# A two-layer hybrid trunk on one core: F16 halves for the value products, an earlier weight split, and memory queries as a seven-product set

## The chip, the core and the metric

The kernel runs on one core of a Trainium2 chip. The time is the device time of one execution in microseconds (us). TensorE (PE) multiplies matrices, with its weight loads as a stream of their own (PEld); VectorE (DVE), ScalarE (ACT) and GpSimd (POOL) do the elementwise work; SyncE (SP) issues the transfers. Each engine works through its own queue in order, and the engines wait for each other by semaphores.

## The reference, cut to what matters

Two residual layers over 2048 tokens of width 1024, then a last RMSNorm. Layer 0 is gated linear attention (GLA), layer 1 dilated window attention; each also attends over 256 memory rows, multiplies by a SiLU gate and projects back.

```
for i in range(DEPTH):                                   # DEPTH = 2
    h = rmsnorm(x, norm_w[i])
    if i % 2 == 0: mix, q_mem, gate = gla_mixer(h, ...)   # 4 heads, Dk = 96, Dv = 192
    else:          mix, q_mem, gate = dilated_mixer(h, w_in_b[j])
    mem_o = memory_attention(q_mem, mem_n, w_memkv[i])    # 4 heads of 64
    branch = concatenate([mix, mem_o]) * silu(gate)
    x = x + branch @ w_out[i]
...
# gla_chunked, chunks of 64 tokens:
q_in, k_in, k_out = q * exp(b), k * exp(-b), k * exp(b_last - b)
A = where(causal, q_in @ k_in.T, 0)
o = A @ v + q_in @ S;   S = exp(b_last) * S + k_out.T @ v
```

## The kernel before

**Products.** A large product takes both operands as a high and a low F16 half and adds three F16 products into one bank (`mm3`: hi x hi, hi x lo, lo x hi; lines 181 to 183). Weights are scaled by a power of two, cast to the high half on ACT, and the low half is the difference on DVE. `proj` does this over the 8 slices of the width (24 matmuls). `F32` matmuls appear in the trace as two instructions.

**Prologue and the loop of layer 0.** The tokens come in 16 blocks of 128 (two chunks each). The prologue loads and splits the input weights (wv2, wv0, wv1, wk1, wqk, wq0; `lw1_steps`) and does the projections of blocks 0 and 1. The loop then runs over b, and in step b: `gla_o(b)` multiplies AT by v and qs by the state S (both f32, lines 644 and 645, into one bank per head pair) and elb (the k_out of the formula) by v for the new state (line 650); the projections of block b+2 (`pre_gl`, `pre_v`, `pre_k`, `pre_qk`, `pre_q`) fill TensorE; `gla_T` and `gla_A` transpose q and k of block b+1 and multiply them (line 635), and a masked copy (`copy_predicated`, line 637) writes AT. `pre_la`, `pre_elb` make cumulated gates with F32R products against `tri` and `rev` (lines 569 to 578) and per-chunk sums against `ind` (f32, line 580). Inside the loop the order on PE, DVE, ACT and POOL is that of the code (`manual_schedule`). Side work is cut into steps, taken in turn by `tick`: the norm of the next block (`ga_steps`), the memory rows (`mem_rows`: two scaled row blocks, line 686, each transposed, line 691), the memory keys and values (`mem_steps`, line 710, in a bank of the projections' pool ps_mm), and in later blocks the weights of the second pass (`w2_steps`).

**Second pass of layer 0.** Over the 16 blocks again: memory query, memory attention (lines 260, 261, 286, 288, with transposes by DMA into mp and mpt), gate, the branch (transposed by DMA into bT), the output projection (`ps_o<-wo,bT`), and the next layer's normed input into h2T (`a2_h2`). In front of the first block the output projection's weights are loaded in four quarters and split. Order here is a scheduler's. `a2_sums` makes combinations S1 to S4 of h2T and stores them.

**Start of layer 1.** From here PE follows the order of the code again. A pair of column blocks of w_in_b is multiplied either directly (`proj_t`: 24 matmuls of 512 columns for a quarter of the tokens) or as a seven-product set (Strassen-like: seven products of 12 matmuls in place of eight for a half of the tokens and 256 columns, with weight combinations T1 to T4 on POOL and the stored S1 to S4 as the other operand). Memory queries take eight `proj_t` (`memq`), gate column block 4 four (`gate4`); between them stand the loads of S, the last sums and the first set's norm, combinations and splits. Then twelve sets follow.

## Time and profile before

| quantity | value |
|---|---|
| runs | 2552.51, 2547.39, 2550.93 us; median 2550.93 us |
| the profiled execution's own time | 2551.06 us |
| its span | 2549.3 us |
| TensorE busy | 2472.3 us, 97% of the span |
| DVE, ACT, POOL busy | 1583.3, 1331.8, 577.5 us |
| prologue, loop of layer 0, second pass's start | 0 to 66, 66 to 437, 437 to 520 us |
| second pass, start of layer 1, sets | 520 to 866, 866 to 966, 966 to 1440 us |
| attention with its projections, end | 1440 to 2350, 2350 to 2549 us |

A row of a timeline gives the start, the time, the engine, line, operation, output and inputs, and in brackets how long the engine sat idle before it and what released it. A row by line gives busy time, mean ns of one, and idle time ahead with its releaser. Stage bounds in the table are where TensorE's work passes from one to the next.

### The profile page before, as it was taken

What the parts mean: (1) busy time and instruction counts of PE and PEld (TensorE: products, weight loads), DVE (VectorE), ACT (ScalarE), POOL (GpSimd) and SP (SyncE); (2) the same over time, 40 slices, a digit from 0 to 9 for tenths busy, and PEclk for the clock granted to TensorE, in tenths of its full rate; (3) what the DMA queues carried; (4) which work ended last, traced back from release to release, by engine and by line L of the source; (5) the groups of instructions that cost most, each with busy time, mean ns of one, the idle gap of its engine ahead of it and who ended that gap; (6) DMA issues with size and microseconds to landing.
All of it is one profiled execution on the core that took longest, in us unless ns stands there. A gap on an engine that the chain in (4) does not pass through costs nothing.

```text
span 2549.3 us, 44543 instructions
## 1 busy us (share of the span) xinstructions
PE 2472.3 (97%) x16801; PEld 1653.3 (65%) x16801; DVE 1583.3 (62%) x3563; ACT 1331.8 (52%) x2905; POOL 577.5 (23%) x471
## 2 busy tenths in 40 slices
PE   7999999999999899999999999999999999998998
PEld 5888988788888744444544455555555555554898
DVE  6444554666875765655655455677776767768643
ACT  6434653544544545755555455556565655555322
POOL 0000000011210223455543012133242323323100
PEclk9999999999999999999999999999999999999999
DMA  6223432456666654568773324376575756748752
GB/s 239 79 86 105 136 112 69 133 145 156 173 166 133 158 187 119 157 162 188 167 201 120 121 56 112 90 169 164 132 183 118 183 133 163 166 124 216 233 180 98
DMA packets 623627, 371.71 MB, mean 146 GB/s; under 512 B 443874, under 2 KB 555956, under 8 KB 623028
## 3 DMA queue, kind: packets, MB, share of 16 engines
q1 hardware_dynamic: 623412, 368.87, 54.7%
q8 instruction: 131, 2.15, 0.4%
q14 instruction: 84, 0.69, 0.1%
HBM read 185.74 MB, written 95.86 MB: 110 GB/s over the span
## 4 chain that ended last, share of the span: by engine, by line
PE 78%; DVE 7%; DMA 6%; ACT 3%; issue 3%; SPq 1%; POOL 1%; DVEq 0%; ACTq 0%; POOLq 0%
PE ps_mm L183 15%; PE ps_mm L181 15%; PE ps_mm L182 15%; PE ps_x L183 6%; PE ps_x L181 6%; PE ps_x L182 6%; PE ps_mm L710 1%; DMA mpt<-stg 1%; PE ps_o L181 1%; PE ps_o L183 1%; PE ps_o L182 1%; PE ps_g L181 1%; PE ps_g L183 1%; PE ps_g L182 1%; PE ps_g L650 1%
## 5 line engine op out<-in xcount | busy, mean ns | idle before, releaser
L181 PE MATMUL ps_mm<-h2T,w 128*128 128x512 f16 x1112 | 423.4, 381 | 4.9 <-ACT w L1138 4.6
L183 PE MATMUL ps_mm<-h2T,w 128*128 128x512 f16 x1112 | 422.7, 380 | 0.6 <-DVE w L1142 0.6
L182 PE MATMUL ps_mm<-h2T,w 128*128 128x512 f16 x1112 | 423.0, 380 | 0.0
L181 PE MATMUL ps_mm<-w,hT 128*128 128x256 f16 (+1 forms) x1408 | 386.0, 274 | 7.8 <-ACT w L429 5.8
L183 PE MATMUL ps_mm<-w,hT 128*128 128x256 f16 (+1 forms) x1408 | 385.7, 274 | 0.0
L182 PE MATMUL ps_mm<-w,hT 128*128 128x256 f16 (+1 forms) x1408 | 385.6, 274 | 0.0
L183 PEld LDWEIGHTS <-w 128*128 128x128 f16 x1952 | 191.5, 98 | 233.7 <-issue 3.3
L181 PEld LDWEIGHTS <-w 128*128 128x128 f16 x1952 | 191.6, 98 | 216.7 <-ACT w L1138 5.2
L182 PEld LDWEIGHTS <-w 128*128 128x128 f16 x1952 | 191.6, 98 | 215.9 <-issue 8.4
L175 POOL TENSOR_TENSOR ph<-pm,ph 128x512 f16<-128x512 f32 (+2 forms) x144 | 162.5, 1128 | 630.7 <-ACT ph L174 427.9
L181 PE MATMUL ps_x<-h2T,w 128*128 128x512 f16 x552 | 210.0, 380 | 1.3 <-DVE c L1366 1.3
L182 PE MATMUL ps_x<-h2T,w 128*128 128x512 f16 x552 | 209.8, 380 | 0.0
L183 PE MATMUL ps_x<-h2T,w 128*128 128x512 f16 x552 | 209.7, 380 | 0.0
L1555 ACT ACTIVATE pm<-pm,st,cols 128x256 f32<-128x256 f32 (+1 forms) x288 | 156.1, 543 | 74.5 <-DVE st L1548 73.7
L175 POOL TENSOR_TENSOR stg<-mp,stg 128x512 f16<-128x512 f32 x16 | 19.5, 1217 | 725.7 <-ACT stg L174 725.7
L1544 DVE CUSTOM_DVE_ANT_0 pm<-ps_g,mw 128x256 f32<-128x256 f32 (+1 forms) x288 | 92.9, 359 | 98.3 <-PE ps_g L183 97.8
L181 PEld LDWEIGHTS <-hT 128*128 128x128 f16 x1408 | 138.2, 98 | 21.5 <-issue 2.2
L182 PEld LDWEIGHTS <-hT 128*128 128x128 f16 x1408 | 138.2, 98 | 20.1 <-issue 2.5
L183 PEld LDWEIGHTS <-hT 128*128 128x128 f16 x1408 | 138.1, 98 | 17.2
L1504 ACT ACTIVATE rx<-rw 128x512 f16<-128x512 f32 x36 | 33.9, 940 | 114.8 <-DVE rw L1503 114.8
L1488 ACT ACTIVATE rx<-ps_mm 32x512 f32<-32x512 f32 x96 | 56.1, 584 | 58.7 <-PE ps_mm L183 25.4
L174 ACT ACTIVATE ph<-pm 128x512 f16<-128x512 f32 (+2 forms) x144 | 77.3, 537 | 4.6
(625 smaller groups left out, 5925.3 us busy)
## 6 DMA issues: line engine op xcount, KB each, us to landing
stg<-in_w_in_b SPq DMA_DIRECT2D x80, 256.0 KB
v<-vd SPq DMA_DIRECT2D x72, 256.0 KB
fb<-fd SPq DMA_DIRECT2D x24, 768.0 KB
od<-osb SPq DMA_DIRECT2D x68, 256.0 KB
og<-od SPq DMA_DIRECT2D x68, 256.0 KB
x<-in_x SPq DMA_DIRECT2D x32, 512.0 KB
stg<-in_w_in_b SPq DMA_DIRECT2D x24, 512.0 KB
vd<-vo SPq DMA_DIRECT2D x48, 256.0 KB
```

The lines of the kernel that those rows point to most:

```text
L174: A.activation(out=hi, in_=src, func=AF.Copy)
L175: G.tensor_tensor(out=lo, in0=src, in1=hi, op=ALU.subtract)
L181: PE.matmul(o, sh, mh, start=first, stop=False)
L182: PE.matmul(o, sh, ml, start=False, stop=False)
L183: PE.matmul(o, sl, mh, start=False, stop=last)
L650: PE.matmul(t[:DK, (h % 2) * DV:(h % 2 + 1) * DV], elb[:, h * DK:(h + 1) * DK], v[:, h * DV:(h + 1) * DV], start=True, stop=True)
L710: PE.matmul(t[:, m * 256:(m + 1) * 256], w[:, k, ms] if j == 0 else memT[:, k, ms], memT[:, k, :] if j == 0 else w[:, k, :], start=k == 0, ...
L1488: A.activation(out=X[r0:r0 + 32, :], in_=t[0:32, :], func=AF.Copy)
L1504: A.activation(out=fold(X.bitcast(F16)[:, 0:512], g), in_=perm(W, g), func=AF.Copy, scale=SQ)
L1544: V.tensor_tensor_reduce(out=pm[:, at:at + w * P], in0=s[:, at:at + w * P], in1=masks["mw" if w == 2 else "mf"], scale=1.0, scalar=NEG, op ...
L1555: A.activation(out=p_, in_=p_, func=AF.Exp, scale=sc, bias=st[:, jc + jj:jc + jj + 1], accum_out=st[:, ns + jc + jj:ns + jc + jj + 1])
```

## The change

**Value products.** v, AT and elb are kept as F16 halves, and AT x v and elb x v are three F16 products each (`mm3`) in place of one f32 product; qs x S stays f32. So that the halves are in range, the projections of v, k and q get common scales (`group_scale`, some two dozen operations on single columns), which the output norm takes back. New are the split of AT (`gla_AT`), of elb (`pre_elb_out`), and of v (`halves`). `gla_A` now stands behind `pre_qk`. The per-chunk sums take the F32R halves lah and lal.

**Memory.** `mem_rows` scales both row blocks ahead of the transposes; `mem_steps` takes its bank from ps_tr.

**Output projection's weights.** Loaded and split as side work of loop steps 0 to 4, stored to DRAM, loaded again (4 x 1 MB) where the second pass begins. The first block's branch is transposed on TensorE, as the last one's was.

**Layer 1's start.** The memory queries are the first of now thirteen sets; the gate's column block takes the room between them and the second pass, which now ends inside this stage (`a2_h2(NB - 1)` behind two of the gate's quarters).

```diff
-                PE.matmul(br[:DK, 384 + 2 * h:386 + 2 * h], d["la"][:, h * DK:(h + 1) * DK], ind, start=True,
-                          stop=True)
+                hs_ = slice(h * DK, (h + 1) * DK)
+                PE.matmul(br[:DK, 384 + 2 * h:386 + 2 * h], d["lah"][:, hs_], ind, start=True, stop=False)
+                PE.matmul(br[:DK, 384 + 2 * h:386 + 2 * h], d["lal"][:, hs_], ind, start=False, stop=True)
+        def halves(hl, src, sc):
+            A.activation(out=hl[:, 0], in_=src, func=AF.Copy, scale=sc)
+            V.scalar_tensor_tensor(out=hl[:, 1], in0=src, scalar=sc, in1=hl[:, 0], op0=ALU.mult, op1=ALU.subtract)
...
+            if early:
+                d["v2"] = tl(k1, [P, 768], F32, "og")[:, :256]
+                A.activation(out=d["v2"], in_=p0[:, :256], func=AF.Copy)
+            else:
+                halves(v[:, :, 512:768], p0[:, :256], vsc[:, 2:3])
...
+        def pre_elb_out(d):
+            eh = tl(k1, [P, 2, 384], F16, "eh")
+            A.activation(out=eh[:, 0], in_=d["elb"], func=AF.Copy)
+            V.tensor_tensor(out=eh[:, 1], in0=d["elb"], in1=eh[:, 0], op=ALU.subtract)
+            d["elb"] = eh
...
-            AT = d["AT"] = ATs[d["b"] % 2]
             V.copy_predicated(heads(AT), cmask.unsqueeze(1).to_broadcast([P, HA, P]), heads(am))
 
+        def gla_AT(d):
+            d["AT"] = tl(k2, [P, 2, 512], F16, "ATh")
+            A.activation(out=d["AT"][:, 0], in_=AT, func=AF.Copy)
+            V.tensor_tensor(out=d["AT"][:, 1], in0=AT, in1=d["AT"][:, 0], op=ALU.subtract)
...
-                PE.matmul(o, AT[:, h * P:(h + 1) * P], v[:, h * DV:(h + 1) * DV], start=True, stop=False)
+                mm3(o, *[ah[:, y, h * P:(h + 1) * P] for y in range(2)],
+                    *[v[:, y, h * DV:(h + 1) * DV] for y in range(2)], True, False)
...
-                    PE.matmul(t[:DK, (h % 2) * DV:(h % 2 + 1) * DV], elb[:, h * DK:(h + 1) * DK],
-                              v[:, h * DV:(h + 1) * DV], start=True, stop=True)
+                    mm3(t[:DK, (h % 2) * DV:(h % 2 + 1) * DV], *[elb[:, y, h * DK:(h + 1) * DK] for y in range(2)],
+                        *[v[:, y, h * DV:(h + 1) * DV] for y in range(2)], True, True)
...
-                mt, r = mts[:, m, :], rs[m]
-                V.scalar_tensor_tensor(out=mt, in0=mt, scalar=r, in1=mnw, op0=ALU.mult, op1=ALU.mult)
-                yield
+                mt = mts[:, m, :]
+                V.scalar_tensor_tensor(out=mt, in0=mt, scalar=rs[m], in1=mnw, op0=ALU.mult, op1=ALU.mult)
+            yield
+            for m in range(2):
+                mt = mts[:, m, :]
...
-                t = bank(ps_mm)
+                t = bank(ps_tr)
...
+                wo.append(inv)
+                SY.dma_start(wo_d[j], wt)
...
+        def group_scale(dst, ds, f, g):
+            top, rt = col(), tl(sp, [P, 1], F32, "ws")
+            V.tensor_tensor(out=top, in0=ds[0]["inv"], in1=ds[1]["inv"], op=ALU.max)
+            if len(ds) > 2:
+                V.tensor_tensor(out=top, in0=top, in1=ds[2]["inv"], op=ALU.max)
+            V.reciprocal(rt, top)
+            for j, d in enumerate(ds):
+                V.tensor_scalar(out=dst[:, j:j + 1], in0=d["inv"], scalar1=rt, scalar2=f, op0=ALU.mult, op1=ALU.mult)
+                if g != 1.0:
+                    V.tensor_scalar(out=dst[:, j:j + 1], in0=dst[:, j:j + 1], scalar1=g, scalar2=None, op0=ALU.mult)
+            V.tensor_scalar(out=top, in0=top, scalar1=1.0 / f, scalar2=None, op0=ALU.mult)
+            tops.append(top)
+
+        for d in (d0, d1):
             for _ in lw1_steps(d):
                 pass
         setup_w()
+        group_scale(vsc, (d0, d1, d2), 2.0 ** -13, 1.0)
+        for _ in lw1_steps(dk):
+            pass
+        rest = [lw1_steps(d) for d in (dqk, dq)]
+        for g_ in rest:
+            next(g_)
+            next(g_)
+        group_scale(ksc, (dk, dqk), 2.0 ** -13, 1.0)
+        group_scale(iqs, (dq, dqk), 2.0 ** -25, DK ** -0.5)
+        for g_ in rest:
+            for _ in g_:
+                pass
...
+            if 1 <= b < 5:
+                act.append(w2_steps(wor, b - 1))
+            if b < 4:
+                wor = wo_load(b)
...
-            if m:
-                gla_A(m)
             tick(2)
             if n:
                 pre_qk(n)
+            if m:
+                gla_A(m)
+                gla_AT(m)
+            if n:
                 tick(2)
                 pre_eb(n)
                 pre_k_out(n, "enb")
...
+                pre_elb_out(n)
+            if b == 11:
+                mem0 = load_mem(0, ca, kvi[0], w2[0][1])
...
+        wot = [tl(wo_p, [P, 2, KT, 256], F16, f"wo{j}") for j in range(4)][::-1]
+        for wt, wd in zip(wot, wo_d):
+            SY.dma_start(wt, wd)
...
-            if b + 1 < NB:
+            if 0 < b < NB - 1:
...
-        for j in range(4):
-            wt = tl(wo_p, [P, 2, KT, 256], F16, f"wo{j}")
-            wo.append((wt, load_w(wt, [(0, a["w_out"][0, :, j * 256:(j + 1) * 256])], 256, None,
-                                  (stg, sga)[j % 2], "stg", ps_tr, True)))
...
-        a2_h2(NB - 1, xt)
...
-        sets.insert(1, ("g", 6, 7936))
+        sets[0:0] = [("q", 0, 6912), ("g", 6, 7936)]
         sets += [("g", 0, 7168), ("g", 2, 7424)]
...
-        def memq(c):
-            for pr in range(2):
-                out_q(c, pr, proj_t(wq["w"][pr], c))
-
-        wq = pair_raw([6912, 7040])
-        pair_norm(wq, ps_g, True)
-        for j in range(2):
-            pair_split(wq, j)
-        mem1 = load_mem(1, mc, kvi[1], wq["inv"][0], True)
-        wg4 = pair_raw([GATE2[0]])
-        load_s(slice(0, 4))
-        memq(1)
-        out_q(3, 0, proj_t(wq["w"][0], 3))
+        wg4 = dict(raw=tl(wp, [P, KT, P], F32, "w"), w=[], m=1, c0=GATE2[:1])
+        pair_load(wg4, 0)
         pair_norm(wg4, ps_g)
         pair_split(wg4, 0)
         gneg4 = neg_of(wg4["inv"][0])
+        gate4(1)
+        gate4(0)
+        a2_h2(NB - 1, xt)
+        c2x.close()
+        mc = cv.enter_context(pool("mc", 1))
+        mk = cv.enter_context(pool("mk", 1))
+        qk_ = cv.enter_context(pool("qkp", 2))
+        vv_ = cv.enter_context(pool("vv", 3))
+        svp = cv.enter_context(pool("svp", 1))
+        Ss = {n: tl(svp, [P, 8, 2, 4, P], F16, n) for n in ("S1", "S2", "S4")}
         cur = set_raw(sets[0][2])
-        out_q(3, 1, proj_t(wq["w"][1], 3))
-        gate4(1)
+        load_s(slice(0, 4))
+        gate4(3)
         for x in range(4):
             load_s3(x)
-        gate4(3)
+        set_norm(cur, ps_g)
+        for x in range(1):
+            set_split(cur)
+        for x in ("T1", "T2"):
+            set_diff(cur, x)
         load_s(slice(4, 6))
         for x in range(4, 6):
             load_s3(x)
-        sums(6)
-        memq(0)
-        set_norm(cur, ps_g)
-        for x in ("T1", "T2", "T3", "T4"):
+        for x in range(2):
+            set_split(cur)
+        for x in ("T3", "T4"):
             set_diff(cur, x)
-        sums(7)
-        gate4(0)
         for x in range(4):
             set_split(cur)
-        memq(2)
+        nxt = set_raw(sets[1][2])
+        mem1 = load_mem(1, mc, kvi[1], cur["inv"], True)
         gate4(2)
-        for x in range(3):
-            set_split(cur)
-        nxt = set_raw(sets[1][2])
-        mem_q(0)
```

The first place is the middle of a loop step (block 8) on TensorE, where AT's product of the next block stands (kT, qT; line 635 before, 649 now). Before:

```order
L183 LDWEIGHTS hT_2742
L183 MATMUL ps_mm_3036<-w_512_132_278,hT_2742 128x256
L635 MATMUL ps_g_3061<-qT_3023,kT_3016 128x128 x4
L181 LDWEIGHTS hT_2742
L181 MATMUL ps_mm_3071<-w_256_134_282,hT_2742 128x256
```

Now:

```order
L183 LDWEIGHTS hT_3071
L183 MATMUL ps_mm_3423<-w_256_138_282,hT_3071 128x256
L649 MATMUL ps_g_3448<-qT_3381,kT_3374 128x128 x4
L576 MATMUL ps_g_3459<-lah_3390,tr_125_257 128x384
L577 MATMUL ps_g_3459<-lal_3391,tr_125_257 128x384
```

It stood behind the k projection (w_512) and ahead of the projection of q and k (w_256); now that one is ahead of it too.

The second place is `gla_o` of the same step on TensorE, first head. Before:

```order
L580 MATMUL ps_g_3141<-ind_122_257,la_3004 96x2 x4
L644 MATMUL ps_o_3161<-v_2614,AT_124_261 128x192
L645 MATMUL ps_o_3161<-S_2884,qs_3025 128x192
L644 MATMUL ps_o_3161<-v_2614,AT_124_261 128x192
L645 MATMUL ps_o_3161<-S_2884,qs_3025 128x192
```

Now:

```order
L588 MATMUL ps_g_3500<-ind_260,lah_3390 96x2
L589 MATMUL ps_g_3500<-ind_260,lal_3391 96x2
L181 LDWEIGHTS ATh_3454
L181 MATMUL ps_o_3529<-v_2940,ATh_3454 128x192
L182 LDWEIGHTS ATh_3454
L182 MATMUL ps_o_3529<-v_2940,ATh_3454 128x192
L183 LDWEIGHTS ATh_3454
L183 MATMUL ps_o_3529<-v_2940,ATh_3454 128x192
L664 MATMUL ps_o_3529<-S_3231,qs_3383 128x192
```

One f32 product with AT has become three F16 ones with their own weight loads; the product with S stays.

The third place is the start of layer 1 on TensorE, where the last block's normed input (sg) is transposed into h2T. Before:

```order
L183 MATMUL ps_mm_10814<-h2T_4965,w_10745 128x512
L168 MATMUL ps_tr_10690<-ident_82,sg_10688 128x128 x4
L168 MATMUL ps_tr_10697<-ident_82,sg_10688 128x128 x4
L181 LDWEIGHTS w_10745
L181 MATMUL ps_mm_10814<-h2T_4965,w_10745 128x512
```

Now:

```order
L183 MATMUL ps_mm_11260<-h2T_5565,w_11211 128x512
L168 MATMUL ps_tr_11301<-ident_82,sg_11299 128x128 x4
L168 MATMUL ps_tr_11308<-ident_82,sg_11299 128x128 x4
L181 LDWEIGHTS w_11211
L181 MATMUL ps_x_11344<-h2T_5565,w_11211 128x512
```

Before, the same memory query product (ps_mm_10814, other tokens) went on behind the transposes; now the third quarter of the gate (ps_x_11344, `gate4(3)`) follows, whose tokens take in the block just transposed.

136 lines of the change are left out of this document (76 added, 60 removed).

## The prediction

> **What bounds the kernel now.** I read the page first, its engine shares and its chain of waits, and then the windows cut at the program's stages.
>
> ```profile
> span 2549.3 us, 44543 instructions
> PE 2472.3 (97%) x16801; PEld 1653.3 (65%) x16801; DVE 1583.3 (62%) x3563; ACT 1331.8 (52%) x2905; POOL 577.5 (23%) x471
> PE 78%; DVE 7%; DMA 6%; ACT 3%; issue 3%; SPq 1%; POOL 1%; DVEq 0%; ACTq 0%; POOLq 0%
> ...
> 0.00:66.00 66.00, 46.00 (x357) 38.09 (x358) 44.77 (x93) 41.24 (x81) 3.89 (x20) 0.97 0.67 231
> 66.00:437.00 371.00, 363.58 (x2930) 326.81 (x2928) 172.75 (x389) 175.71 (x463) 0.00 (x0) 0.99 0.34 101
> 437.00:520.00 83.00, 75.67 (x654) 66.41 (x655) 56.38 (x141) 43.50 (x94) 5.67 (x5) 0.98 0.39 117
> ...
> 866.00:966.00 100.00, 89.76 (x472) 46.45 (x471) 64.80 (x100) 49.53 (x87) 21.32 (x15) 0.96 0.57 177
> ```
>
> (In the windows' rows stand the window, its length, the busy time of PE, PEld, DVE, ACT and POOL with their instructions, the granted clock, the DMA share and GB/s.) TensorE bounds it: 97% busy, 78% of the chain. So two things shorten the kernel: fewer TensorE microseconds in a full stage, or a TensorE gap closed. The gaps lie where the change works: 20 us in the prologue (0 to 66), 7.4 in the first layer's loop (66 to 437), 7.3 at the second pass's start, 10.2 where the next layer begins (866 to 966). DVE and ACT are at 47% of the loop, so added vector work fits there on average; what counts is whether it is on time.
>
> Durations of single matmuls overstate their cost, because they overlap; the step from start to start is the cost.
>
> ```profile
> 280.17 0.76 PE L580 MATMUL ps_g<-ind,la 128*96 128x2 f32 x8
> 280.80 0.57 PE L644 MATMUL ps_o<-v,AT 128*128 128x192 f32 x2
> ...
> 281.53 0.49 PE L644 MATMUL ps_o<-v,AT 128*128 128x192 f32 x2
> 281.86 0.49 PE L645 MATMUL ps_o<-S,qs 96*128 96x192 f32 x2
> ...
> 283.49 1.46 PE L650 MATMUL ps_g<-v,elb 128*96 128x192 f32 x8
> 284.79 0.28 PE L181 MATMUL ps_mm<-w,hT 128*128 128x272 f16 x1
> 284.91 0.28 PE L182 MATMUL ps_mm<-w,hT 128*128 128x272 f16 x1
> ...
> 1499.92 0.22 PE L182 MATMUL ps_o<-pt,v 128*128 128x128 f16 x1
> 1499.98 0.22 PE L183 MATMUL ps_o<-pt,v 128*128 128x128 f16 x1
> ...
> 1500.20 0.38 PE L181 MATMUL ps_x<-h2T,w 128*128 128x512 f16 x1
> 1500.42 0.38 PE L182 MATMUL ps_x<-h2T,w 128*128 128x512 f16 x1
> ```
>
> An f32 product of 192 columns is two instructions and 0.33 us (281.53 to 281.86); eight for elb take 1.30 (283.49 to 284.79). In F16 128 columns cost 0.06, 272 cost 0.12, 512 cost 0.216. So 192 cost about 0.082, an estimate between the first two.
>
> **Part 1, value products.** Per block four AT and four elb products go from 4 x 0.33 + 1.30 = 2.62 us to 24 x 0.082 = 1.97: -0.65, times 16 blocks -10.4 us. The ind products become eight F32R calls in place of four f32 calls of two instructions: 0.63 us for eight (280.17 to 280.80), so nothing if an F32R call is one instruction, +0.63 x 16 = +10 if it is two. I take nothing: the trace has the tri products, F32R already, as one row each.
>
> The new work is the split of AT, between the masked copy and gla_o; the split of elb, which is used a whole block later; and the halves of v.
>
> ```profile
> 275.67 0.73 DVE L637 COPY_PREDICATED AT<-cmask,ps_g 128x512 f32<-128x512 int32 x1
> ...
> 275.31 1.05 ACT L739 ACTIVATE w<-stg 128x1024 bf16<-128x1024 f32 x1
> ...
> 898.19 1.29 DVE L998 TENSOR_TENSOR h2T<-ps_tr,h2T 128x512 f16<-128x512 f32 x2
> ...
> L1189 ACT ACTIVATE S<-c x6: 629/630/630, 928.7 to 953.9; 128x512 f16<-128x512 f32 x6
> ```
>
> The chain is 0.73 + 0.63 (ACT cast) + 0.65 (DVE difference) = 2.0 us, near 2.3 with handovers. gla_A now stands behind the first of the two last projections: ahead of gla_o remain 24 matmuls at 0.11, two tri pairs at 0.43 and the ind products, 4.1 us. In front of the cast ACT has two L739 passes, the second done at 276.4, while the masked copy moves from 275.7 to about 278.3. So I cost it at nothing; without that cover it would be 2.3 us a block.
>
> **Part 2, memory rows and memory products.** Both scalings now come ahead of the transposes, and the L710 products use another bank.
>
> ```profile
> 95.29 1.09 PE L691 MATMUL ps_tr<-ident,stg 128*128 128x128 f32 x4 [3.55 <-DVE stg L686]
> 96.17 0.85 PE L644 MATMUL ps_o<-v,AT 128*128 128x192 f32 x2
> 96.81 0.85 PE L645 MATMUL ps_o<-S,qs 96*128 96x192 f32 x2
> ...
> L710 PE MATMUL ps_mm<-stg,stg 128*128 128x256 f32 x128 | 28.6, 381 | 2.2 <-DVE elb L588 2.2
> ```
>
> After the idle 3.55 us the products run at half speed (0.64 a pair instead of 0.33) until about 100.5, 2 us more. Of 5.6 I take -5, a remainder staying for the second scaling's end; and -2.2 for the waits on L588, as ps_tr is not held by elb.
>
> **Part 3, prologue.** It gets some 23 column operations (0.15 us each, 3.5), halves for two blocks (six at 0.42, 2.5), two elb differences and one AT difference (0.65 each): 8 us more DVE.
>
> ```profile
> 41.13 0.16 DVE L425 TENSOR_TENSOR cols<-cols 128x1 f32<-128x1 f32 x1
> ...
> 55.14 0.84 DVE L588 SCALAR_TENSOR_TENSOR enb<-ps_mm,cols,enb 128x256 f32<-128x256 f32 x2 [3.21 <-ACT enb L573]
> ...
> 62.40 0.35 DVE L588 SCALAR_TENSOR_TENSOR enb<-ps_mm,cols,enb 128x128 f32<-128x128 f32 x1 [5.12 <-PE ps_mm L183]
> ```
>
> DVE, which splits the weights TensorE waits for, has 44.8 busy us in these 66; 8.3 of its idle time lie late, in these two waits. Bounds: 0 if the idle time takes it, +8 if none. The AT split at the tail (1.3) is exposed anyway; I take +4.
>
> **Part 4, start of the second pass.** The output projection's weights are split in blocks 1 to 4, stored and loaded again (4 MB); block 15's products are mixed with the second pass's first projections; the first bT comes by eight TensorE transposes.
>
> ```profile
> 437.23 0.59 PE L644 MATMUL ps_o<-v,AT 128*128 128x192 f32 x2 [0.81 <-DVE AT L637]
> ...
> 482.73 0.39 PE L181 MATMUL ps_o<-wo,bT 128*128 128x256 f16 x1 [4.27 <-DMA bT<-og]
> ...
> GB/s 0 222 311 268 382 410 117 75 236 370 353 381 385 386 385 384 424 414 412 426 377 390 416 256 16 0 9 222 77 0 0 0 95 204 92 218 0 0 0 0
> ```
>
> Removed are the 4.27, the clock lost behind it (0.02 of the window's 83 us, 1.7), and of the window's other idle time (7.33 - 4.27) and the 0.81 of L644 some 2.5; added are the eight transposes, 0.9 (four took 95.29 to 96.17 at half clock). That is -7.6; I take -7. The reload takes 4 MB / 390 GB/s = 10.5 us and stands ahead of the first memory transposes on SP; some 28 us of projections (about 260 matmuls at 0.11) lie in front of the first use, so nothing. If the transposes or the first use wait for it, at most +10.5.
>
> **Part 5, memory queries.** Eight products of 24 matmuls become fourteen of 12: 24 fewer at 0.216, -5.2 us.
>
> **Part 6, start of the next layer.** That set now stands first, and the 41 us that the queries used to lie over its loads are gone; the gates stand there instead.
>
> ```profile
> 887.28 0.61 PE L181 MATMUL ps_mm<-h2T,w 128*128 128x512 f16 x1 [4.61 <-ACT w L1138]
> 888.89 0.61 PE L183 MATMUL ps_mm<-h2T,w 128*128 128x512 f16 x1 [0.57 <-DVE w L1142]
> 889.29 0.63 PE L181 MATMUL ps_mm<-h2T,w 128*128 128x512 f16 x1
> ...
> 949.53 0.38 PE L181 MATMUL ps_x<-h2T,w 128*128 128x512 f16 x1 [1.30 <-DVE c L1366]
> ...
> 962.97 0.38 PE L181 MATMUL ps_x<-S,w 128*128 128x512 f16 x1 [2.90 <-DVE c L1366]
> ```
>
> These waits are 9.4 us, and the half clock (0.40 from 888.89 to 889.29, a step that else takes 0.216) some 2.9 of the window's 4.0 (0.04 of 100 us): 12.3 go. New ones come. The gate's split may be 1 us late. Block 15's transposes wait about 0.5. Behind them gate 3 needs all of that block's h2T at once: 0.63 + 1.29, with handovers 2.5 us, where before another query product stood. The first set's evacuations queue behind the sums: 2 us as at 962.97. Together 6, so -6.3. The clock decides little: after 2.90 us of idle the step was not halved, after 3.55 it was.
>
> The Trainium skill ("TensorE: Matmul & The Clock Gate", Part 1) puts the limit at one idle window of about 3.4 us; the two rows agree, and by it the 2.5 costs no half clock, which would add some 1.7.
>
> **The sum.** -10.4 - 5 - 2.2 + 4 - 7 - 5.2 - 6.3 = -32.1 us from the profiled execution's 2551.06 (span 2549.3, 1.8 around it; the median of the runs is 2550.93): **2519 us**.
>
> **The rivals.**
> *A: the conv start starves.* The S loads wait for the output projection's last read, and those of S2 stand on SP behind the stores of block 15's h2T; 4.5 MB at 390 GB/s are 11.5 us, but at this window's mean of 177 they are 25. Cover from gate 3 to the second product: 5.2 + 5.2 + 2.6 = 13. Stall 12 and half clock 2: 2533. Against it: S1 and S2 come first, and they are 2 MB.
> *B: 96-column weights.* If F16 loads of 96 columns don't hide, each of elb's 12 products takes the 0.16 that an f32 one takes: 16 x 12 x 0.08 = +15, 2534. Against it: eight loads of 96 columns in 0.63 at L580, 0.079 each, just under 0.082.
> The Trainium skill (same page, "Weight-path perf modes") keeps its fast weight load to 128 columns. No run here shows an F16 load of 96.
> *C: F32R calls are two instructions.* +10, 2529.
> *D, the other side: gla_o waits for AT in every block.* ACT and DVE are in-order; if the cast stands behind the two L739 passes (2.1) and two exponentials (about 1), it comes 3 us late against a margin of 4.1 - 2.3 = 1.8, and with a late masked copy more. Each block's wait above 2.1 us eats the whole gain (32 / 15); at 2.5 it is 2519 + 37 = 2556, at 3 with half clock behind it (1.5 more) 2519 + 67 = 2586; at 2, the turning point, 2549. For it: the waits of L644 on L637 at 437.23, where no cover was. Against it: block 8's times above. A mild form, 1 us a block, gives 2534.
>
> **Chances.** The forecast 0.72, A 0.08, B 0.04, C 0.04, D mild 0.05, D at its turning point 0.02, D full 0.05. The likeliest case's own range comes from its bounds: prologue 0 to +8, conv start -12 to +3 and memory rows -5.6 to -3 against what I took, 2509 to 2531. To hold 8 in 10 it reaches up past A, B, C and mild D: 2508 to 2538. No change would be within 0.2%, 5 us, about what a measurement of this kernel can tell: that takes a loss of 27 us against the sum: D at its turning point, and 0.03 for A twice as long, 0.05; slower is D full, 0.05; faster 0.90.
>
> **What would show it.** A step of about 0.08 for products from ATh and eh, and 2 us for a block's 24. No wait above 1 us at the memory transposes or the L710 products. The first output projection without a wait on DMA. A wait of 2 to 3 us at gate 3, none above 4 at the first set. Prologue's end at about 69 us instead of 65.5. Wrong would be a wait on ATh in each block, a half clock behind gate 3, or a loop stage as long as the 371 us of before.

## The result: faster by 14 us, where 32 were forecast

The changed kernel takes 2535.8 us (median, 2533.82 to 2539.84) against 2549.47 (2547.39 to 2552.51) before: a ratio of 0.9947, 95% interval [0.9934, 0.9959]. The direction was right and the time lies inside the range; the gain is 13.7 us where 32.1 were forecast.

The page of the changed kernel, its span and its engines:

```profile
span 2534.4 us, 44922 instructions
PE 2453.6 (97%) x16913; PEld 1640.3 (65%) x16913; DVE 1631.7 (64%) x3673; ACT 1359.2 (54%) x2957; POOL 593.8 (23%) x478
```

TensorE is still 97% busy. Its busy time fell by 18.7 us, DVE's rose by 48. Windows cut at the starts of `gla_o(0)` and `gla_o(14)` and at the first output projection show the loop and the stretch behind it, before first, then after (window, its length, busy PE, PEld, DVE, ACT and POOL, granted clock, DMA share, GB/s):

```profile
65.00:422.00 357.00, 350.38 (x2853) 314.95 (x2853) 166.94 (x374) 171.89 (x449) 0.00 (x0) 0.99 0.33 98
422.00:483.00 61.00, 53.67 (x411) 47.71 (x410) 32.63 (x88) 23.92 (x60) 2.27 (x2) 1.00 0.40 126
```

```profile
68.00:408.00 340.00, 337.21 (x2976) 302.90 (x2976) 213.73 (x464) 206.53 (x508) 0.00 (x0) 0.99 0.41 123
408.00:468.00 60.00, 54.08 (x429) 47.50 (x428) 29.73 (x81) 19.09 (x52) 2.27 (x2) 0.97 0.50 167
```

The loop lost 17 us and is nearly gapless (337.2 of 340). The stretch from `gla_o(14)` to the first output projection is as long as it was. The starts of the same work in the traces, in us, tell it whole (first AT product of a block; first product of attention, `ps_g<-k,q`, behind the last set). The other kernels are told below:

| kernel | gla_o(0) | gla_o(14) | from there to first k,q | first k,q | span |
|---|---|---|---|---|---|
| before | 65.5 | 422.6 | 1054.5 | 1477.1 | 2549.3 |
| after | 67.7 | 407.9 | 1053.6 | 1461.5 | 2534.4 |
| products in f32 (u3) | 63.7 | 406.2 | 1048.6 | 1454.8 | 2525.2 |
| halves from block 3 on (v1) | 63.6 | 401.9 | 1057.7 | 1459.6 | 2532.8 |
| memory rows back (u2) | 68.9 | 428.1 | 1050.9 | 1479.0 | 2551.7 |
| f32 and memory rows back (y1) | 63.6 | 414.4 | 1050.8 | 1465.2 | 2538.4 |
| weights back (u1) | 68.6 | 404.5 | 1068.9 | 1473.4 | 2548.5 |
| query in another bank (x5) | 68.4 | 408.6 | 1047.4 | 1456.0 | 2528.4 |
| f32 and other bank (w1) | 64.2 | 406.6 | 1041.9 | 1448.5 | 2522.1 |

At `gla_o(14)` the changed kernel is 14.7 us ahead; the forecast's parts for this stretch come to 12.3 (14 blocks at 0.65, the memory rows' 7.2, less 4). Behind it, where the forecast has another 19.8, 0.9 arrived up to the first k,q product, and 0.7 were lost after it. Traces of kernels with the same code in a stretch differ there by 2.5 us at `gla_o(0)` (67.3 to 69.8), by 4.5 at `gla_o(1)` (94.6 to 99.1) and by some 3 in the second pass, where the waits on the transfers of memory attention (mp) come to 6.9 us from 470 to 840 us in the changed kernel's trace and to 2.6 to 5.0 in four others (e1, x5, u4, u6). Single entries are read no finer than that.

The rows that the forecast named, in the loop of the changed kernel:

```profile
293.53 0.17 PE L588 MATMUL ps_g<-ind,lah 128*96 128x2 f32 x1
...
294.15 0.26 PE L181 MATMUL ps_o<-v,ATh 128*128 128x192 f16 x1
294.25 0.25 PE L182 MATMUL ps_o<-v,ATh 128*128 128x192 f16 x1
294.33 0.25 PE L183 MATMUL ps_o<-v,ATh 128*128 128x192 f16 x1
...
296.57 0.25 PE L181 MATMUL ps_g<-v,eh 128*96 128x192 f16 x1
...
297.57 0.28 PE L181 MATMUL ps_mm<-w,hT 128*128 128x272 f16 x1
```

The eight F32R calls take 0.62 us (293.53 to 294.15), one instruction each; the step of an F16 product of 192 columns is 0.08 (294.25 to 294.33), and elb's twelve, whose weights have 96 columns, take 1.00 (296.57 to 297.57), 0.083 each. There is no wait on ATh in the loop behind block 0. The second pass's start, SP, ACT, DVE and TensorE:

```profile
436.35 1.85 SPq L996 DMA_DIRECT2D wo<-wod  x4
...
452.32 0.72 ACT L305 ACTIVATE e<-e,cols 128x512 f32<-128x512 f32 x1
452.94 0.38 ACT L237 ACTIVATE qm<-ps_mm 128x256 f16<-128x256 f32 x1
453.35 0.42 DVE L238 SCALAR_TENSOR_TENSOR qm<-ps_mm,qm 128x256 f16<-128x256 f32 x1 [0.44 <-ACT qm L237]
...
453.83 0.27 PE L181 MATMUL ps_mm<-w,hT 128*128 128x256 f16 x1 [3.13 <-DVE qm L238]
...
454.37 0.42 PE L183 MATMUL ps_mm<-w,hT 128*128 128x256 f16 x1
...
457.78 0.28 PE L181 MATMUL ps_mm<-w,hT 128*128 128x256 f16 x1
```

The 4.27 us on the branch's transfer are gone. In their place TensorE waits 3.13 us for the evacuation of block 1's memory query (L237, L238), which stands in ACT's queue behind block 0's memory exponentials and a gate's passes, and 0.95 on the same operation for block 0; and from 454.37 to 457.6 its steps are 0.21 us instead of 0.11, another 1.6 lost. The start of layer 1:

```profile
858.40 1.97 PE L168 MATMUL ps_tr<-ident,sg 128*128 128x128 f32 x8 [3.45 <-DVE sg L1033]
...
908.89 0.38 PE L181 MATMUL ps_x<-h2T,w 128*128 128x512 f16 x1 [2.41 <-DVE c L1336]
912.97 0.38 PE L181 MATMUL ps_mm<-h2T,w 128*128 128x512 f16 x1 [1.32 <-DVE c L1336]
...
925.98 0.38 PE L181 MATMUL ps_mm<-S,w 128*128 128x512 f16 x1 [1.51 <-DVE c L1336]
932.65 0.38 PE L181 MATMUL ps_mm<-h2T,w 128*128 128x512 f16 x1 [1.33 <-DVE c L1336]
```

The 4.61 us on the query weights are gone too; the transposes of block 15's branch wait 3.45 us for its gating, and the first sets wait 6.6 us for their own evacuations. So the question was why the gain behind the loop was given back, and whether the loop's gain is what it was taken for.

### The profile page after: what moved, and what is told of

Its sections match the earlier page's. It is cut to its first block, busy times and chain, and to the rows that moved or that the text cites. A ratio compares the mean times of both kernels' runs of the same rounds, so it can differ in the third digit from the quotient of the medians.

```text
span 2534.4 us, 44922 instructions
## 1 busy us (share of the span) xinstructions
PE 2453.6 (97%) x16913; PEld 1640.3 (65%) x16913; DVE 1631.7 (64%) x3673; ACT 1359.2 (54%) x2957; POOL 593.8 (23%) x478
## 5 line engine op out<-in xcount | busy, mean ns | idle before, releaser
L181 PE MATMUL ps_mm<-h2T,w 128*128 128x512 f16 x1092 | 414.9, 380 | 3.3 <-DVE c L1336 2.7
L182 PE MATMUL ps_mm<-h2T,w 128*128 128x512 f16 x1092 | 414.9, 380 | 0.0
L183 PE MATMUL ps_mm<-h2T,w 128*128 128x512 f16 x1092 | 414.8, 380 | 0.0
L181 PE MATMUL ps_mm<-w,hT 128*128 128x256 f16 (+1 forms) x1408 | 386.5, 275 | 12.9 <-ACT w L429 6.0
L181 PE MATMUL ps_x<-h2T,w 128*128 128x512 f16 x540 | 204.7, 379 | 2.7 <-DVE c L1336 2.4
L182 PE MATMUL ps_x<-h2T,w 128*128 128x512 f16 x540 | 204.7, 379 | 0.3 <-DVE h2T L1085 0.3
L183 PE MATMUL ps_x<-h2T,w 128*128 128x512 f16 x540 | 204.7, 379 | 0.0
L175 POOL TENSOR_TENSOR stg<-mp,stg 128x512 f16<-128x512 f32 x16 | 18.5, 1156 | 718.4 <-ACT stg L174 718.4
L181 PE MATMUL ps_mm<-S,w 128*128 128x512 f16 x208 | 78.8, 379 | 1.5 <-DVE c L1336 1.5
```

The lines of the kernel that those rows point to most:

```text
L175: G.tensor_tensor(out=lo, in0=src, in1=hi, op=ALU.subtract)
L181: PE.matmul(o, sh, mh, start=first, stop=False)
L182: PE.matmul(o, sh, ml, start=False, stop=False)
L183: PE.matmul(o, sl, mh, start=False, stop=last)
```

## The experiments

Each is timed beside the kernel before, on the same chip; "13.7 below" means below it by medians.

### Four edits at the new waits (e1 to e4)

At first I took three rows for three separate causes. e1 moves one 1024-column scaling from DVE to POOL, which in the trace idles DVE 1.94 us at 451.73 for a transfer behind the 4 MB reload:

```diff
-        V.tensor_scalar(out=nw1, in0=nw1, scalar1=nws1, scalar2=None, op0=ALU.mult)
+        G.tensor_scalar(out=nw1, in0=nw1, scalar1=nws1, scalar2=None, op0=ALU.mult)
```

> The change, but the scaling of the next layer's norm weights (128x1024, in front of the second pass) is done on POOL instead of DVE. Theory: the row nwb is loaded behind the 4 MB reload, DVE waits 1.94 us for it and everything behind it in DVE's queue comes late, so TensorE waits 3.1 us for qm. Then this wait goes and the time falls by about 3 us (2535.8 to 2533, ratio to the kernel before 0.9936). Rival: the next thing, the first memory transposes or the reload itself, is just as late; then the 3.1 us come back behind another releaser and the time stays (0.9947).

Measured: 2537.03, 13.8 below, ratio 0.9942 [0.9923, 0.996]. The wait on qm (the query's halves) is the same 4.1 us in two pieces: DVE was not late here, ACT was (the rows above).

e2 takes the gate's power-of-two scale from h2T instead of from its own weights, so that its split does not wait for their DMA:

```diff
...
-        pair_norm(wg4, ps_g)
+        pair_sq(wg4, h2T[:, 0, :, 0:P])
+        pair_sum(wg4, ps_g)
+        pair_scale(wg4)
```

> The change, but the power of two that scales the gate's column block is taken from a block of h2T and not from the block's own weights (that norm is left out), so that no ACT instruction waits for the block's load ahead of block 15's gate. Theory: ACT waits 2.9 us for that load with the gate's last exponential behind it, so block 15's branch and its transposes (L168, idle 3.45 us) come late. Then the 3.45 us shrink to under 1 and the time falls by about 3 us (0.9936). Rival: the chain of block 15 on DVE (row maximum, token scale, branch) is what is late; then the wait at L168 stays above 2.5 us and the time stays.

Measured: 2537.91, 12.9 below, 0.9949 [0.9934, 0.9964]. Groups of waits from 840 to 945 us:

```profile
PE ps_tr L120 <- DVE rb L118: 3.2, 1, 3.2
...
PE ps_mm L183 <- DVE w L1222: 1.5, 1, 1.5
PE ps_tr L168 <- DVE sg L1033: 1.5, 1, 1.5
```

The 3.4 us on sg L1033 became 1.5; in their place stand 1.5 on the gate's split and 3.2 on the next set's norm, where the changed kernel has 0.8. e3 puts the two sums behind the first and third product of the first set:

```diff
-        sums(6)
-        sums(7)
...
+                    if n == 0 and cc == 0 and i in (1, 3):
+                        sums(6 + i // 2)
```

> The change, but the last two sums (of token blocks 6 and 7 of each half) are written behind the first and third product of the memory queries' set instead of ahead of the set. Theory: the first set's evacuations (added, on DVE) queue behind the sums; the four waits on them (2.4 + 1.3 + 1.5 + 1.5 us, 6.6 in all) shrink to under 2.5 and the time falls by 4 us (0.9931). Rival: the sums are needed 18 us later for the second half's products, and DVE has no room for both; then the waits move to the second half and the time stays within 1 us (0.9947).

Measured: 2541.76, 9.0 below, 0.9967 [0.9955, 0.9979]: worse by some 5 us. The L1336 waits are gone, but the products that need the sums wait for them, and from 910 to 940 the granted clock is 0.83:

```profile
PE ps_mm L182 <- DVE S L1264: 3.8, 1, 3.8
PE ps_mm L181 <- ACT S L1263: 3.4, 1, 3.4
```

e4 is the three together.

> The three edits of the other runs together. Theory: the three waits are independent, one behind the other on TensorE's path, so their gains add: 3 + 3 + 4 = 10 us, 2526, ratio 0.9908. Rival: one of them only hides another (the first of them sets when later loads start), so the sum is under 6 us, ratio above 0.9923.

Measured: 2544.32, 6.5 below, 0.9974 [0.9961, 0.9986]. Nothing adds up. What follows from the four: e1's row was not what TensorE waited for, in e2 the next links took most of the wait that was removed, and in e3 the waits moved to the sums themselves and grew.

### The parts undone one at a time (u1 to u4, u6)

u1 loads and splits the output projection's weights at the second pass's start again:

```diff
-            if 1 <= b < 5:
-                act.append(w2_steps(wor, b - 1))
-            if b < 4:
-                wor = wo_load(b)
...
+            wo.append(load_w(wt, [(0, a["w_out"][0, :, j * 256:(j + 1) * 256])], 256, None,
+                             (stg, sga)[j % 2], "stg", ps_tr, True))
```

> The changed kernel with one part undone: the output projection's weights are loaded and split at the start of the second pass again, as before the change; the first block's branch stays with its eight transposes on TensorE. The prediction put 7 us on this start (4.3 of a DMA wait, 1.7 of half clock, 2.5 of small waits, less 0.9). Theory 1 (these waits passed to the next link, the memory scores' chain, where the changed kernel's trace shows 3.13 us on DVE qm): undoing it costs 0 to 3 us, 2536 to 2539. Theory 2 (the early split does save what was predicted, and the loss is elsewhere): +5 to +8, 2541 to 2544.

Measured: 2550.81, 1.8 above before, 1.0012 [1.0002, 1.0022], so some 15 us slower than the changed kernel: twice the prediction's value, and far from my theory. The waits between 424 and 485 us:

```profile
PE ps_mm L181 <- DVE ws L124: 4.5, 1, 4.5
PE ps_mm L181 <- DVE qm L238: 4.1, 2, 3.1
PE ps_tr L120 <- DVE rb L118: 3.2, 1, 3.2
```

The wait on qm is the same, and the weights' own scale chain (rb, ws) comes on top, with a granted clock of 0.93 from 404 to 485 us. Before the change no wait on these splits stood at this place. What is different since: `gla_o(15)` follows `gla_o(14)` after 19.98 us, before the change after 14.64. Work of 5.3 us that used to cover the second pass's start now stands ahead of it. With the memory products in their old bank (u2, y1 below) the interval is 14.75 and 14.64, so it is part 2 that moves this work. That this is what exposes u1's splits is likely and was not tried. The trace also shows a price of the early split that the prediction left out: without it the steps of blocks 1 to 4 are shorter by 0.1, 0.8, 0.8 and 0.8 us (22.68, 22.70, 29.68 and 29.69), 2.5 in all.

u3 keeps v, AT and elb in f32 and multiplies them in f32:

```diff
...
-                mm3(o, *[ah[:, y, h * P:(h + 1) * P] for y in range(2)],
-                    *[v[:, y, h * DV:(h + 1) * DV] for y in range(2)], True, False)
+                PE.matmul(o, ah[:, h * P:(h + 1) * P], v[:, h * DV:(h + 1) * DV], start=True, stop=False)
...
```

> The changed kernel with the value products in f32 again: v, AT and elb are kept as f32, four AT and four elb products a block, no halves and no cast of AT; everything else stays. Theory 1 (the product term is real: the trace has the AT and elb products at 42.3 us before and 32.2 after, and a block's step of the loop 0.94 us shorter): +9 to +13 us, 2545 to 2549. Rival (what the products save in the loop is given back by the loop's vector work, so that the loop's gain comes from the memory rows): +2 to +5, 2538 to 2541.

Measured: 2529.41, 19.6 below, 0.9926 [0.9911, 0.9941]: *faster* than the changed kernel by 6 us, against both expectations. The first products of block 0, and the issue of the reload, in this kernel:

```profile
63.72 0.59 PE L656 MATMUL ps_o<-v,AT 128*128 128x192 f32 x2 [0.88 <-DVE AT L646]
...
406.47 1.78 SPq L989 DMA_DIRECT2D wo<-wod  x4
```

and in the changed kernel:

```profile
67.69 0.26 PE L181 MATMUL ps_o<-v,ATh 128*128 128x192 f16 x1 [1.55 <-ACT ATh L654]
```

The halves put the first block off by 4.0 us, and lengthen its step from 25.10 to 28.03; 1.7 of that is half clock (0.94 granted in these 28 us), which u4 and u6, with the same code up to there, don't show (26.37 and 26.38). A block's step is shorter by 0.52 in block 1 and by 0.51 to 0.58 in the nine blocks 5 to 13 (23.39 against 22.81, 5.1 us in all); in blocks 2 to 4, two of which (30.38 against 30.49) carry the memory products, it is longer by 0.1 to 0.2. There TensorE waits, in the changed kernel, for the square sums of the output projection's weights (from 66 to 408 us):

```profile
PE ps_tr L105 <- DVE rb L771: 1.6, 3, 0.5
```

These waits of 0.5 us a block are in neither u3's trace nor u1's, so it takes both the halves and the early split to make them. The differences add up to +4.0 + 2.9 - 0.5 + 0.4 - 5.1 = +1.7 at `gla_o(14)`, as in the table: up to there the F16 products cost about as much as they bring.

Behind `gla_o(14)` u3 gains another 5.0. Its reload is issued right behind `gla_o(14)`, 30 us earlier than at 436.35, but that is not shown to be the reason. TensorE waits the same 4.1 us on qm in u3, and the first output projection starts 59.4 us behind `gla_o(14)`, against 59.9. Of the two kernels with the memory part undone (u2 and y1, below) the one with f32 products also issues the reload there and the other 25 us later, and both take 1050.8 us from `gla_o(14)` to the first k,q. Where the 5.0 come from is open. Why the issue moves (less memory held by the halves, most likely) was not tried.

u4 transposes the first block's branch by DMA again:

```diff
-            if 0 < b < NB - 1:
+            if b + 1 < NB:
                 A.activation(out=hl[:, 0:D], in_=sg, func=AF.Copy)
```

> The changed kernel with the first block's branch transposed by DMA again, as before the change; the output projection's weights are still split in the loop. The prediction put the wait of 4.27 us and 1.7 us of half clock on this transfer, less 0.9 for the transposes: +5, 2540 to 2542. Theory 1 (the memory scores' chain stands in front in any case, and the transfer lies beside it): within 1.5 us, 2534 to 2537.

Measured: 2538.61, 12.7 below, 0.995 [0.9935, 0.9965], within 1 us of the changed kernel. The eight transposes are worth nothing that can be told. TensorE does wait 2.9 us for the transfer in u4, beside 3.1 on the query, and its first output projection starts 65.9 us behind `gla_o(14)` instead of 59.9; by block 12 of the second pass the two kernels are level (380.9 and 381.0 us behind it).

u2 undoes the memory part:

```diff
...
-            yield
-            for m in range(2):
-                mt = mts[:, m, :]
...
+                yield
...
-                t = bank(ps_tr)
+                t = bank(ps_mm)
```

> The changed kernel with part 2 undone: each half of the memory rows is scaled and transposed in turn, and the memory products take the other bank again. The prediction put 7.2 us on it, 2541 to 2544 here; by the changed kernel's trace the waits at these places fell from 5.8 us to 0.8, the same. Rival (with the halves' vector work in block 0 the waits would stand there anyway): within 2 us, 2534 to 2538.

Measured: 2555.39, 4.1 above before, 1.0022 [1.0012, 1.0032], so 18 us slower than the changed kernel, more than twice the forecast's value. y1 undoes the same with the products in f32 besides:

> The changed kernel with the value products in f32 and part 2 undone too. Theory 1 (part 2 is worth the predicted 7.2 us by itself, and 19 only where the halves' vector work makes elb, which holds the bank, late): 6 to 9 us slower than the f32 kernel's 19.6 below before, 10 to 14 below. Rival (part 2 is worth 19 in any case): within 3 us of before.

Measured: 2544.42, 6.1 below, 0.9974 [0.9965, 0.9983]. That is 13.5 less than u3's 19.6, more than expected; but in the loop the expected size is there: `gla_o(14)` at 414.4 against 406.2, 8.2 us. The waits from 66 to 408 us, u2 first, then y1:

```profile
PE ps_mm L731 <- DVE elb L596: 6.4, 2, 3.2
PE ps_tr L712 <- DVE stg L707: 4.9, 2, 4.4
```

```profile
PE ps_tr L705 <- DVE stg L700: 3.6, 1, 3.6
PE ps_mm L724 <- DVE elb L595: 2.2, 2, 1.1
```

Without halves the bank's wait is 2.2 us and the memory rows' 3.6, the numbers of before. With the halves' vector work ahead of them the same waits are 6.4 and 4.9, and half clock follows (0.93 granted from 96 to 215 us). So the memory part is worth the predicted size alone, and over twice that (428.1 - 407.9 = 20.2 at `gla_o(14)`) beside the halves: it removes a wait that the halves would have made.

u6 undoes the query set and the order at layer 1's start:

```diff
-        sets[0:0] = [("q", 0, 6912), ("g", 6, 7936)]
+        sets.insert(1, ("g", 6, 7936))
...
+        def memq(c):
+            for pr in range(2):
+                out_q(c, pr, proj_t(wq["w"][pr], c))
```

> The changed kernel with parts 5 and 6 undone: the memory queries are eight products ahead of the first set again, the gates and sums stand where they stood before, and block 15's h2T is formed at the end of the second pass. The prediction put 11.5 us on these parts: 2546 to 2549. Theory 1 (TensorE's work falls by 5.6 us, but the waits at the start of the next layer are only changed for others): +4 to +7, 2540 to 2543. Rival (the queries' cover was worth as much as their work): within 2 us of 2536.

Measured: 2538.01, 13.3 below, 0.9954 [0.9937, 0.997]: no difference to the changed kernel that can be told, against the prediction's 11.5 and my 4 to 7. From `gla_o(14)` to the first k,q it takes 1054.0 against 1053.6. The set saves 24 products, 5.2 us at 0.216 a step. From block 14's output projection (839.7 us) to its first k,q u6 has TensorE busy for 608.8 us of 621.0; the changed kernel has it busy for 602.4 of 619.8 from 841.7, so it idles 17.4 us in place of 12.2: the saved work is given back as waits.

### What holds the first sets (x1, x3, x6)

DVE is busy 42.1 of the 45 us from 895 to 940, so it looked like the new bound there:

```profile
895.00:940.00 45.00, 37.63 (x174) 16.57 (x172) 42.14 (x55) 26.16 (x45) 25.48 (x15) 1.00 0.44 142
```

x1 leaves out the last sums and copies h2T in their place:

```diff
-            x21 = f32q(1, 0, x, G)
-            s = f32q(1, 1, x, V)
...
+            for n in ("S1", "S2", "S4"):
+                for hl in range(2):
+                    SY.dma_start(Ss[n][:, x, hl], quad(1, 0, hl, x))
```

> The changed kernel with the two last groups of sums (6 and 7) left out at the start of the next layer: their S1, S2 and S4 are plain copies of h2T's halves, by DMA, and S3 is not formed, so part of the result is not computed. DVE loses some 15 us of the 48.5 that it is busy between 895 and 945 us of the trace, POOL 13. Theory 1 (DVE is what this stretch waits for: its in-order queue holds the evacuations L1336 behind sums and splits, 6.6 us of TensorE waits): these waits go, 5 to 9 us with the half clock behind them, 2527 to 2531. Rival (the stretch is set by the loads and the weight splits, or by the mpt transfers of the memory products, and DVE is only busy): within 2 us, 2534 to 2538.

Measured: 2534.86, 14.1 below, 0.9951 [0.9936, 0.9965]. The L1336 waits are gone and another stands in their place:

```profile
914.62 0.16 PE L120 MATMUL ps_tr<-rb,ones 128*128 128x1 bf16 x1 [6.91 <-DVE rb L118]
```

This is the norm of the second set's weights, whose loads stand on SP behind eleven of my twelve copies: they are issued 12.7 us behind the first product with S, in the changed kernel 5.0. So the run could not tell the theories apart. x6 leaves them out too, and loads other sums early in their place:

```diff
+        for n_, t_ in Ss.items():
+            SY.dma_start(t_[:, 6:8], s_d[n_][:, 4:6])
...
-        sums(6)
-        sums(7)
```

> The changed kernel with the sums of groups 6 and 7 left out at the start of the next layer: their S1, S2 and S4 are loaded from groups 4 and 5 with three more transfers, early on, and S3 is not formed, so part of the result is not computed. Unlike the earlier run without sums nothing stands in front of the second set's weights on SP. Theory 1 (DVE's load holds TensorE in the first set): the L1336 waits go, 5 to 9 us, 19 to 23 below before. Rival (the second set's weights, from DMA over the square sums to their split, hold the end of the first set in any case): within 2 us of the changed kernel, 12 to 16 below before, with a wait of some us on DVE rb in place of those on L1336.

Measured: 2533.48, 17.2 below, 0.9939 [0.992, 0.9959], between the two. TensorE's only wait group from 895 to 940 in it:

```profile
PE ps_tr L120 <- DVE rb L118: 5.3, 1, 5.3
```

Fourteen microseconds of DVE work less (28.0 busy of the 45 us from 898 to 943; this trace runs some 3 us later) and 6.6 of waits on L1336 gone, but 5.3 come back on the next set's weights. By medians that is 3.5 us better than the changed kernel, which the intervals don't tell from none; the trace is of the slowest of its four runs (2541.93). So DVE's load is at most a part of what holds these sets; behind it stands the chain of the second set's load, square sums and split.

x3 forms sum group 6 in the second pass:

```diff
-SUMS_AT = (6, 8, 10, 12, 13, 14)
+SUMS_AT = (6, 8, 10, 12, 13, 14, 15)
...
```

> The changed kernel with group 6 of the sums formed in the second pass, after block 14's h2T, stored and loaded like groups 0 to 5; only group 7 stays at the start of the next layer. Nothing is left out. Theory 1 (DVE bounds the first set): it loses some 7 us of DVE work from the stretch of 895 to 945 us, where DVE is full, and gets it where DVE is busy 9 to 11 of 15 us; the L1336 waits shrink by half, 2 to 5 us faster, 2531 to 2534. Rival: as the runs with edits of this stretch so far, the wait is passed on to block 15's chain (h2T of block 15 queues behind the sums on DVE), 2535 to 2540.

Measured: 2538.94, 10.1 below, 0.9962 [0.9948, 0.9976]. The L1336 waits fell from 6.6 to 1.2 us, and block 15's last transposes waited 5.4 us for their norm (sg L1071), which now queued behind the sums on DVE. Passed on again.

### Halves only where they pay (v1, v2)

v1 keeps f32 products in blocks 0 to 2:

```diff
+            v = d["v"] = tl(k1, [P, 2, 768], F16, "v") if d["b"] >= 3 else tl(k1, [P, 1, 768], F32, "v")
...
         def pre_elb_out(d):
+            if d["b"] < 3:
+                return
```

> The changed kernel with the value products of blocks 0 to 2 in f32 and of blocks 3 to 15 as F16 halves; all else as in the changed kernel. Theory 1 (the F16 products gain 0.58 us a block where the loop is full, as the steps 23.39 against 22.81 of the two traces show, and lose 7 us at the start, where the vector work of the halves stands in front of the first blocks: first gla_o at 63.7 against 67.7, second at 88.8 against 95.7): both gains together, 2521 to 2526. Rival (the start's gain is given back in the loop, or what the f32 kernel won lies behind the loop): 2529 to 2534.

Measured: 2535.51, 15.8 below, 0.994 [0.9923, 0.9956]. In the loop theory 1 holds: `gla_o(14)` at 401.9, 4.3 ahead of u3 and 6.0 ahead of the changed kernel. Behind the loop all of it is lost: 1057.7 to the first k,q against u3's 1048.6. The start of its second pass, TensorE and then DVE:

```profile
449.54 0.37 PE L181 MATMUL ps_mm<-w,hT 128*128 128x256 f16 x1 [4.78 <-DVE qm L238]
```

```profile
447.27 0.75 DVE L1145 TENSOR_SCALAR nwb<-nwb,cols 128x1024 f32<-128x1024 f32 x1 [3.41 <-DMA nwb<-in_norm_w]
```

The norm weights come behind the 4 MB reload, DVE idles 3.41 us, and the evacuation of the query queues behind that. But this wait is not where v1 loses its 9 us on u3: counted from `gla_o(14)`, it is 3.6 behind at the first output projection, level at block 10 of the second pass (328.0 us in both), 4.0 behind at the first product with S, and 9.1 at the first k,q. v2 is v1 with e1's edit.

> The kernel with F16 halves from block 3 on (15.8 below before), with the scaling of the norm weights moved from DVE to POOL. In that kernel's trace DVE idles 3.41 us on this row's DMA, behind the 4 MB of the output projection, and TensorE waits 4.78 on DVE qm. Theory 1 (the reload holds the queue): the wait falls to the 3.1 of the changed kernel and the half clock goes, 2 to 3.5 us, 18 to 19.5 below before. Rival (the exponentials on ACT end as late): within 1 us, 15 to 17 below.

Measured: 2533.27, 17.4 below, 0.9927 [0.9911, 0.9944], between the two expectations. TensorE's longest wait on qm falls from 4.78 to 3.1 us, as theory 1 says, and the time by 1.6, which the intervals don't tell from none. The norm weights behind the reload held v1 for that long; behind them stand ACT's exponentials, as in the changed kernel. To the first k,q it takes 1058.0 us all the same. What costs v1 and v2 the time further on is open.

### The query's bank (x5, v3, w1)

x5 changes one bank:

```diff
-            pq = bank(ps_mm)
+            pq = bank(ps_x if b == 1 else ps_mm)
```

> The changed kernel with the memory query of block 1 in another PSUM bank (ps_x, idle there), so that block 0's second gate does not wait for that query's evacuation and the query's matmuls stand earlier, in the gap around the memory products. Theory 1 (the 3.13 us wait on DVE qm took the place of the 4.27 us wait on the branch, and it is a matter of one bank): it goes, with the half clock behind it, 3 to 5 us: 13.7 below before becomes 17 to 19 below. Rival (the next link, the transfers of the memory scores, takes it): within 2 us of the changed kernel, 12 to 16 below before.

Measured: 2529.59, 21.1 below, 0.9914 [0.9899, 0.9929]: 7 us faster than the changed kernel, more than the 3 to 5 expected. The waits from 427 to 468 us, and the first and last of the query's 24 matmuls:

```profile
PE ps_mm L181 <- DVE sg L310: 2.2, 1, 2.2
PE ps_tr L733 <- DVE p2e L97: 1.0, 1, 1.0
...
440.26 0.27 PE L181 MATMUL ps_x<-w,hT 128*128 128x256 f16 x1
...
442.77 0.27 PE L183 MATMUL ps_x<-w,hT 128*128 128x256 f16 x1
```

The query's products now stand ahead of ACT's exponentials, in the gap that used to be a wait; nothing waits on qm, and no half clock follows. v3 is this with v2's edits.

> The same with the memory query of block 1 in the other bank besides: F16 halves from block 3 on, norm weights scaled on POOL, query of block 1 in ps_x. Nothing is left out. Theory 1: the three gains add, 20 to 24 below before, faster than the changed kernel by 6 to 10. Rival (each wait is passed on): 14 to 18 below before.

Measured: 2529.63, 21.0 below, 0.992 [0.9904, 0.9936], no faster than x5 alone. Its loop ends 6 us earlier (402.6), and from there to the first k,q it takes 1051.9 where x5 takes 1047.4. Of the 4.5, 2.5 are there at the first product with S and the rest comes behind it; the causes were not separated. w1 is x5 with the products in f32:

> The changed kernel with the value products in f32 and the memory query of block 1 in ps_x; nothing is left out. Theory 1 (the two gains are in different places, the loop's first blocks and the second pass's start): 22 to 25 below before, the fastest so far. Rival (the later start of the memory chain eats the second, as for the kernel with halves from block 3 on): 18 to 21 below.

Measured: 2524.58 (2523.67 to 2526.33), 26.0 below, 0.99 [0.9883, 0.9916]: the fastest of all, 12 us ahead of the changed kernel, and the two gains add (6 and 7). Its only wait group from 427 to 468 us:

```profile
PE ps_tr L726 <- DVE p2e L97: 0.9, 1, 0.9
```

## Why the prediction was right and wrong

**Where the gain is missing.** Up to `gla_o(14)` 2.4 us more came than was forecast; behind it 0.2 of the 19.8. So the failed steps are Parts 4, 5 and 6, which stood for 18.5 of these. All three counted a removed wait, or removed work, at its full length as time; the runs show that the next producer was late by nearly as much.

**The sum up to the loop's end was right by luck, its terms were not.** 12.3 were forecast at `gla_o(14)` and 14.7 came. But of these the F16 products (Part 1, with the halves' share of Part 3) are no gain: +1.7, where -9.1 and +4 stood in the sum. The price of the product was right: 0.08 a step, and 0.58 a block in a full block against the 0.65 forecast. The sum took that price 16 times, and up to `gla_o(14)` it holds in ten blocks of fourteen. In blocks 2 to 4 it is nothing, as the waits on the early split's square sums eat it, and in block 0 and the prologue the halves' vector work is on the path (+6.9, 5.2 without the half clock; I had put +4 for the whole of Part 3, and u3, which keeps the scale columns, has its first `gla_o` 1.8 us ahead of before, so the columns cost nothing that shows). It is the two terms named next that brought the sum to its size: -8.2 for Part 2, -8.2 uncounted, and the +1.7 make the 14.7.

**Part 2** is worth 8.2 alone, forecast 7.2. That it would be worth 20 beside Part 1 was not seen: I priced each edit against the kernel before, not against the kernel with the other edits in it.

**Not in the sum** is another 8.2 us at `gla_o(14)` which y1, without Parts 1 and 2, has against before (414.4, 422.6): the step falls from 23.75 to 23.39, the first steps from 30.65 and 25.98 to 28.32 and 25.34. Left in y1 are the place of `gla_A`, the second buffers for kT and qT, and the order around `pre_v_out`, which I cost at nothing. Which of them it is was not tried, but the traces of block 8 say where most of the step's 0.36 us lies: around the products of qT and kT. From the last projection product ahead of them to the first product behind them it takes 1.24 us before (272.74 to 273.98) and 0.92 in y1 (269.35 to 270.27). That points to `gla_A`'s place or its buffers.

**Part 4 failed, at "Removed are the 4.27, the clock lost behind it".** The wait was removed, but behind it stood the evacuation of the next query, late by nearly as much: 3.13 and 0.95, with 1.6 of half clock. I asked what is late next only for the reload and named a price for that alone (0 to 10.5). u4 shows the transposes to be worth nothing that can be told, x5 that the one bank was worth 7. The early split also costs 2.5 us in the loop (u1), a term that the sum does not have. Beside the other edits the split is worth more than the 7 put on it (u1: 15), likely because Part 2 moved its cover.

**Part 5 was right as work and wrong as time**: 24 products fewer, the 5.2 us of the forecast, and nothing of it in the time (u6).

**Part 6 failed, at "so -6.3".** The old waits went as said; gate 3 waits 0.6 us, not 2.5. The terms for the new ones were too small where it counted: "block 15's transposes wait about 0.5" is 3.45 with half clock behind it, and "the first set's evacuations queue behind the sums: 2 us" is 6.6. Without the 41 us of cover one chain of weights, sums, splits and evacuations fills this stretch, and of six edits to it (e2, e3, x1, x3, x6, u6) none brought a gain that the intervals tell from none. Further on, in the sets, the waits on the transfers of memory attention (mpt) grew from 0.8 to 3.6 us, which the sum does not have either.

**The rivals.** A did not happen as such: no product waits for the S loads. B and C are excluded by the rows at 293 to 298 us (0.083 us a product with 96-column weights, eight F32R calls in 0.62). D is excluded in the loop; its wait is there where no cover was, in the prologue (1.55 at 67.69). What came true is none of them: behind the loop each removed wait uncovered another of nearly its size.

**Two readings of the prediction are wrong in themselves.** "After 2.90 us of idle the step was not halved" looked at the first microsecond only; the clock was halved after that (the rows are in the last section), so the two rows do not agree with a limit between them, and a wait of 2.5 us could not be taken as free of half clock. And the bounds of the likeliest case add up to 2534 at the top (4 + 9.3 + 2 above 2519), not 2531; the wide range holds both.

## What to carry to other kernels

A removed wait is worth the distance to the next producer's end, not its own length: at a place without cover, list what else TensorE waits for there, and what the second-latest ends at, before counting the gap as gained. Price each edit of a bundle against the kernel that has the others in it, since one edit may only repair what another breaks. Work that makes matmuls cheaper with more vector work paid here in the full steady blocks, and cost at the pipeline's start, where the same vector work is on the path.
